# Conditioning vector and its row products begin within the first mixer, with a sum buffer of their own

## The chip, the core and the metric

One core of a Trainium2 chip runs the whole program. The metric is device time in microseconds (us) of one execution; the median of the runs counts. The engines are named as in the profile: PE is TensorE (PEld its weight loads), DVE VectorE, ACT ScalarE, POOL GpSimd, SP SyncE, whose queue issues most DMAs.

## What is computed

Two transformer blocks on 512 tokens of width 1024, in float32, one after the other:

```python
x = first_block(x, mem, ...)      # mixer (two attentions), cross attention, SwiGLU
x = second_block(x, c, ...)       # mLSTM mixer, squared-ReLU MLP, MLA mixer, squared-ReLU MLP
# in second_block
cond = jax.nn.silu(c)             # one vector of 1024
for l in range(2):
    ada = cond @ ada_w[l] + ada_b[l]               # 6 rows of 1024
    sh1, sc1, g1, sh2, sc2, g2 = jnp.split(ada, 6, axis=-1)
    ...
kv_shift, kv_scale = jnp.split(cond @ kv_ada_w + kv_ada_b, 2, axis=-1)
```

The 14 rows of 1024 (six per layer and two for the shared keys and values) depend on c and on weights alone, on nothing of the first block. They are first needed at the end of SwiGLU, and from there on until the last MLP.

## The kernel before

The stream x stays on chip. Each weight matrix comes in by SP's DMA queue, is split by ACT and DVE into a rounded high part and a low rest, and every product is three PE matmuls (high by high, high by low, low by high: `prod`, L440, lines L445 to L447). A wino product (L490) with seven instead of eight block products serves the later blocks of the squared-ReLU MLPs; it asks DVE for sums beside the splits. Instructions are written out in program order; a list scheduler then orders each engine's queue by that order and by its own estimate of when operands and buffers are there, and puts in the waits. On the chip each engine works its queue in that fixed order, so an instruction whose operand is late holds all behind it.

The stages in the order of time: first mixer (value projection, then 64 softmax tiles of `soft64` woven with projections, then the output projection) until 346 us, cross attention until 500, SwiGLU until 850, mLSTM until 1100, first squared-ReLU MLP until 1450, MLA until 1700, second squared-ReLU MLP until the end. Between two stages stands a `boundary` (L641), a chain over normalisation and transposes.

**The rows in the background.** `cond` (L793) loads c and makes silu(c) with a Tanh on ACT and two small DVE instructions. `ada` (L804) is a generator that makes the rows, each in two halves of 512 columns by `row_by` (L838). One half is nine steps: POOL clears a sum tile and fetches the bias (L843, L844); eight slices of weights (256 KB each) come into two `araw` slots by SP's queue (L856), and for each DVE does sum = slice * cond + sum (L852); DVE adds the two halves of the partitions (L860), ACT and DVE split the result into `hl` (L864); one PE matmul with ones adds up over the partitions (L869); DVE applies the gain (L882 or L886), and POOL sends the half row to DRAM (L888, shown as L201, the line of its helper). Two further half-width products (rows 14 and 15) and four fetches of a row as columns belong to the same generator. In all it has 278 steps.

`step` (L453) is called for each product of `prod`, at 0.65 units each, and advances the generator by one step when 3 units are used up (2.5 from the end of mLSTM on): every fifth (fourth) product. Within a boundary (`quiet`) it doesn't. Before `self.bg = self.ada()` it has nothing to advance. `crow` (L893) and `gcol` (L406) advance it at once where a row is needed and not there.

Buffers by tag: `u2` has 16 slots of 2 KB a partition for all kinds of tiles, `araw` 2, the 8 PSUM banks are `ps`. A tile waits for a free slot of its tag.

Of the kernel before, what the change touches and what calls it, by code (L numbers as in the profile page):

```python
# [10 lines left out]
F32 = mybir.dt.float32  # L11
F32R = mybir.dt.float32r
# [8 lines left out]
P = 128  # L21
# [9 lines left out]
D_FF = 2816  # L31
ALL = slice(0, S)

BUF = dict(s8=14, u2=16, row=3, raw=4, w0=4, w1=4, w2=4, w3=5, w4=5, w5=5, w6=5, w7=5, ps=8, pace=3, pacb=2.5, man=0, lag=3, lagx=3, lagm=3, half=1, quiet=1, xp=0, fp=2, r1=1.25, r1b=3.6, r1c=2.4, r2=1.6, r2b=2.6, rx=1.4, rm=0.6, pre=10, gl=3, pl=0, hb=300, hs=0, ha=0, sp=0, spq=1.3, sq=1, b1=1, b2=1, lc=7, mb=(6, 8, 6, 6, 6), mc=(4, 3, 4, 4, 4), st2=1, pr2=8, z1=4.5, z2=5, gt=3, rv=2, gs=1, rl=3, n1=4, ex=2, em=3, vg=1, sb=(8, 8, 6), mo=4, x1=2, g0=20, st=1, y1=0, y2=1, y3=0, ph=2, pq=0, fy=1, u1=6, s32=4, sm=60)

TWO_PI = 2.0 * np.pi

# [101 lines left out]
class Net:  # L139
# [27 lines left out]
    def big(self, shape, dt=F32):  # L167
        return self.t("s8", shape, dt, BUF["s8"])

    def u2(self, shape=(P, S), dt=F32):  # L170
        if BUF["u1"] and int(np.prod(shape[1:])) <= 256:
            return self.t("u1", shape, dt, BUF["u1"])
        return self.t("u2", shape, dt, BUF["u2"])

    def row(self, n=DM):
        return self.t("row", [P, n], F32, BUF["row"])

    def sm(self, n=1, p=P, dt=F32):
        if n > 8:
            return self.t("sm32", [p, n], dt, BUF["s32"])  # L180
        return self.t("sm", [p, n], dt, BUF["sm"])
# [656 lines left out]
    def row_by(self, i, c, ws, n, vec, b=None, gain=None, kind=0):  # L838

        nc, V = self.nc, self.nc.vector  # L840
        acc = self.u2((P, n))
        if b is not None:
            nc.gpsimd.memset(acc, 0.0)  # L843
            self.small(acc[0:1, :], b.rearrange("(o c) -> o c", o=1))  # L844
        yield
        raws = {}
        for k in range(0, KD + 2, 2):
            for j in (k, k + 1):
                if j == 2 and b is None:
                    V.tensor_scalar(out=acc, in0=raws.pop(0), scalar1=vec[:, 0:1], scalar2=None, op0=ALU.mult)  # L850
                elif j >= 2:
                    V.scalar_tensor_tensor(out=acc, in0=raws.pop(j - 2), scalar=vec[:, j - 2:j - 1], in1=acc,  # L852
                                           op0=ALU.mult, op1=ALU.add)
                if j < KD:
                    raws[j] = self.t("araw", [P, n], F32, 2)
                    nc.sync.dma_start(out=raws[j], in_=ws[:, j, :])  # L856
            yield
        if BUF["fy"]:
            h = P // 2
            (V if BUF["fy"] == 1 else nc.gpsimd).tensor_tensor(out=acc[0:h, :], in0=acc[0:h, :], in1=acc[h:P, :], op=ALU.add)  # L860
            hl = self.u2((P, n), F32R)
            for _ in range(BUF["y1"]):
                yield
            self.parts(hl[0:h, :], hl[h:P, :], acc[0:h, :])  # L864
            yield
            for _ in range(BUF["y2"]):
                yield
            ps = self.bank((P, n))
            nc.tensor.matmul(ps, lhsT=self.onesr, rhs=hl, start=True, stop=True)  # L869
        else:  # L870
            hi, lo = self.u2((P, n), F32R), self.u2((P, n), F32R)
            for _ in range(BUF["y1"]):
                yield
            self.parts(hi, lo, acc)
            yield
            for _ in range(BUF["y2"]):
                yield
            ps = self.bank((P, n))
            nc.tensor.matmul(ps, lhsT=self.onesr, rhs=hi, start=True, stop=False)
            nc.tensor.matmul(ps, lhsT=self.onesr, rhs=lo, start=False, stop=True)  # L880
        if gain is None:
            V.tensor_copy(out=acc[0:1, :], in_=ps[0:1, :])  # L882
        else:
            g = self.u2((1, n))
            self.small(g, gain.rearrange("(o c) -> o c", o=1))
            V.scalar_tensor_tensor(out=acc[0:1, :], in0=ps[0:1, :], scalar=1.0 if kind == 1 else 0.0,  # L886
                                   in1=g, op0=ALU.add, op1=ALU.mult)
        self.small(self.arow[i:i + 1, c:c + n], acc[0:1, :])  # L888
        if c or n < S:
            self.have.add(i)  # L890
        yield
# [157 lines left out]
    def mixer1(self):  # L1049
# [18 lines left out]
        with self.in_order():  # L1068
            self.mixer1_values(h, vf, w)
        self.cap(0)  # L1070

        wg = self.weights(w, 0, KD, 1536, 8, gain="mix")
        psg = self.bank()
# [44 lines left out]
        vs, os, st = [vf, None], [None, None], {}  # L1118
# [9 lines left out]
        def fill():  # L1128
            m = self.mem_in()
            for pair in range(8):  # L1130
                c = 0 if pair < 4 else 1544
                r = []
                if pair == 4:
                    self.cap(1)
                    yield from v_chunk()
                for i, y in enumerate(self.stacks(w, h, c + 512, c, pair % 4, 1.0, 0.125, r, "mix")):
                    if pair == 7 and i in (2, 9):
                        next(m)
                    yield y
                st[2 * pair], st[2 * pair + 1] = r  # L1140
            for _ in m:
                pass
            yield from self.mem_keys()
# [12 lines left out]
        f, gs = fill(), self.gains()  # L1156
# [33 lines left out]
        g = self.brow(a["g_mix_post"][0], eng=self.nc.sync)  # L1190
# [727 lines left out]
    def mixer1_and_tables(self):  # L1918
        r = self.mixer1()
        self.rope_tables()  # L1920
        self.cond()
        self.bg = self.ada()
        return r


# [34 lines left out]
```

## Time and profile before

| | |
|---|---|
| median of 3 runs | 2031.46 us (2030.95 to 2033.41) |
| the profiled execution: time | 2033.3 us |
| its span | 2031.5 us |
| PE, PEld busy in it | 1941.8 us (96%), 1665.1 us (82%) |
| DVE, ACT, POOL busy | 1396.7 us (69%), 1025.0 us (50%), 331.7 us (16%) |
| mean granted PE clock | 0.982 |

All that follows is of the one profiled execution; us in a row count from the start of its span. PE is near its peak over the span as a whole, so that what matters are the few places where it waits.

### The profile page before, as it was taken

The page shows a single profiled execution, that of the slowest core. Times are in us where ns is not written, and L with a number is a line of the kernel's source. Part 1 is how long each engine was busy: PE and PEld are TensorE (multiplying, and loading weights), DVE is VectorE, ACT ScalarE, POOL GpSimd, SP SyncE. Part 2 cuts the span into 40 slices and gives each one's busy share as a digit, 9 for nine tenths or more (in the row PEclk, how much of TensorE's full clock was granted, in tenths as well). Part 3 has the DMA queues.
Part 4 walks back from the last instruction along what each step waited for, and adds up shares of the span by engine and source line. Part 5 has one row for each costly group of instructions (what it writes and reads, how often), then busy time and mean ns, then how long its engine had stood idle before and what let it go on. Part 6 is the DMA issues. An engine that isn't in the chain of part 4 may idle for free.

```text
span 2031.5 us, 29708 instructions
## 1 busy us (share of the span) xinstructions
PE 1941.8 (96%) x10684; PEld 1665.1 (82%) x10684; DVE 1396.7 (69%) x2659; ACT 1025.0 (50%) x2283; POOL 331.7 (16%) x615
## 2 busy tenths in 40 slices
PE   8999998999999999999998899999979999999998
PEld 5888987778888888778888788798767978989987
DVE  5756645756576576757767897889758656657666
ACT  7767874545244233347534363454545644545444
POOL 1321113003000000421126100000330034000001
PEclk9999999999999999999999999999989999999999
DMA  7322341433465465244333355555342203233322
GB/s 219 89 79 76 118 129 61 137 104 103 157 202 159 137 203 142 83 142 129 120 104 113 117 163 156 183 167 159 102 134 89 73 12 103 83 104 115 103 74 83
DMA packets 191667, 245.14 MB, mean 121 GB/s; under 512 B 20059, under 2 KB 119488, under 8 KB 191520
## 3 DMA queue, kind: packets, MB, share of 16 engines
q1 hardware_dynamic: 185264, 232.15, 37.0%
q0 software_dynamic: 6256, 11.10, 1.9%
q8 instruction: 84, 1.38, 0.3%
q14 instruction: 63, 0.52, 0.1%
HBM read 241.00 MB, written 2.20 MB: 120 GB/s over the span
## 4 chain that ended last, share of the span: by engine, by line
PE 69%; DVE 14%; issue 6%; DMA 5%; ACT 4%; POOL 2%; DVEq 0%; POOLq 0%; ACTq 0%
PE ps L447 18%; PE ps L446 18%; PE ps L445 18%; PE ps L508 7%; DMA araw<-in_ada_w 3%; DVE u L852 2%; DVE s L308 2%; DVE s L318 2%; PE ps L1011 1%; DVE s L634 1%; DVE s L342 1%; DVE x L654 1%; ACT junk L579 1%; PE ps L1793 1%; PE ps L1822 1%
## 5 line engine op out<-in xcount | busy, mean ns | idle before, releaser
L445 PE MATMUL ps<-s,s 128*128 128x512 f32 (+4 forms) x2260 | 857.8, 383 | 8.4 <-ACT s L633 4.8
L446 PE MATMUL ps<-s,s 128*128 128x512 f32 (+4 forms) x2260 | 850.5, 377 | 12.2 <-DVE s L634 11.9
L447 PE MATMUL ps<-s,s 128*128 128x512 f32 (+4 forms) x2260 | 845.2, 377 | 4.7 <-DVE s L634 4.6
L446 PEld LDWEIGHTS ps<-s,s 128*128 128x128 f32 (+1 forms) x2260 | 431.7, 191 | 90.0 <-DVE s L634 13.7
L447 PEld LDWEIGHTS ps<-s,s 128*128 128x128 f32 (+1 forms) x2260 | 430.2, 190 | 86.7 <-DVE s L634 7.4
L445 PEld LDWEIGHTS ps<-s,s 128*128 128x128 f32 (+1 forms) x2260 | 429.7, 191 | 84.9 <-ACT s L633 7.5
L508 PE MATMUL ps<-s,s 128*128 128x256 f32 x2184 | 265.3, 282 | 10.0 <-DVE u L524 6.9
L508 PEld LDWEIGHTS ps<-s,s 128*128 128x128 f32 x2184 | 262.8, 189 | 13.8 <-issue 5.9
L852 DVE SCALAR_TENSOR_TENSOR u<-araw,cond,u 128x512 f32<-128x512 f32 x224 | 177.2, 791 | 108.6 <-DMA araw<-in_ada_w 87.2
L308 DVE TENSOR_TENSOR s<-raw,s 128x512 fp32r<-128x512 f32 x277 | 193.3, 736 | 42.5 <-ACT s L307 37.0
L307 ACT ACTIVATE s<-raw 128x512 fp32r<-128x512 f32 x255 | 144.9, 622 | 152.8 <-PE ps L447 96.4
L317 ACT ACTIVATE s<-raw,cols_all 128x256 fp32r<-128x256 f32 (+1 forms) x283 | 134.2, 547 | 47.5 <-issue 22.1
L318 DVE SCALAR_TENSOR_TENSOR s<-raw,cols_all,s 128x256 fp32r<-128x256 f32 (+1 forms) x305 | 150.5, 546 | 8.7 <-ACT s L317 7.3
L201 POOL DMA_DIRECT2D arow<-u x30 | 14.7, 492 | 629.6 <-DVE u L886 378.9
L568 POOL TENSOR_SCALAR sm<-sm 128x1 f32<-128x1 f32 x74 | 20.5, 277 | 558.9 <-ACT junk L579 556.1
L634 DVE TENSOR_TENSOR s<-ps,s 128x512 fp32r<-128x512 f32 (+3 forms) x124 | 75.2, 619 | 40.6 <-ACT s L633 39.7
L341 ACT ACTIVATE s<-raw 128x512 fp32r<-128x512 f32 x104 | 62.6, 621 | 67.9 <-PE ps L447 32.9
L634 DVE TENSOR_TENSOR s<-u,s 128x512 fp32r<-128x512 f32 x102 | 69.7, 686 | 39.4 <-ACT s L633 35.8
L633 ACT ACTIVATE s<-u 128x512 fp32r<-128x512 f32 x102 | 63.6, 625 | 64.0 <-DVE u L1403 49.3
L633 ACT ACTIVATE s<-ps 128x512 fp32r<-128x512 f32 (+3 forms) x124 | 65.2, 538 | 38.3 <-PE ps L626 16.1
L341 ACT ACTIVATE s<-u 128x512 fp32r<-128x512 f32 x78 | 48.7, 624 | 61.0 <-DVE u L345 31.6
L342 DVE TENSOR_TENSOR s<-raw,s 128x512 fp32r<-128x512 f32 x104 | 70.5, 682 | 11.0 <-ACT s L341 10.9
(264 smaller groups left out, 2211.7 us busy)
## 6 DMA issues: line engine op xcount, KB each, us to landing
raw<-in_mlp_w SPq DMA_DIRECT2D x128, 512.0 KB, 4.0
araw<-in_ada_w SPq DMA_DIRECT2D x192, 256.0 KB, 3.0
raw<-in_w_gate_up SPq DMA_DIRECT2D x44, 512.0 KB, 4.3
raw<-in_w_in SPq DMA_DIRECT2D x24, 512.0 KB, 4.6
raw<-in_a_w_in SPq DMA_DIRECT2D x24, 512.0 KB, 4.0
raw<-in_w_down SPq DMA_DIRECT2D x22, 512.0 KB, 4.1
raw<-in_w_mem_kv SPq DMA_DIRECT2D x16, 512.0 KB, 3.6
araw<-in_kv_ada_w SPq DMA_DIRECT2D x32, 256.0 KB, 3.1
```

Of the source, the lines that this page charges most:

```text
L307: A.activation(hi[:, sl, cl], src[:, sl, cl], AF.Copy)
L308: f.tensor_tensor(out=lo[:, sl, cl], in0=src[:, sl, cl], in1=hi[:, sl, cl].bitcast(F32), op=ALU.subtract)
L317: A.activation(hi[:, i, :], src[:, i, :], AF.Copy, scale=g)
L318: V.scalar_tensor_tensor(out=lo[:, i, :], in0=src[:, i, :], scalar=g, in1=hi[:, i, :].bitcast(F32), op0=ALU.mult, op1=ALU.subtract)
L341: A.activation(hi, x, AF.Copy)
L445: self.nc.tensor.matmul(ps, lhsT=ah, rhs=bh, start=first and i == 0, stop=False)
L446: self.nc.tensor.matmul(ps, lhsT=ah, rhs=bl, start=False, stop=False)
L447: self.nc.tensor.matmul(ps, lhsT=al, rhs=bh, start=False, stop=last and i == n - 1)
L508: nc.tensor.matmul(ps, lhsT=l[:, k, :], rhs=m[:, k, :], start=first and k == e == 0, stop=k == 3 and e == 2, skip_group_check=True)
L633: self.nc.scalar.activation(hi, x, AF.Copy)
L634: self.nc.vector.tensor_tensor(out=lo, in0=x, in1=hi.bitcast(F32), op=ALU.subtract)
L852: V.scalar_tensor_tensor(out=acc, in0=raws.pop(j - 2), scalar=vec[:, j - 2:j - 1], in1=acc, op0=ALU.mult, op1=ALU.add)
```

## The change

`cond()` is called, and the generator set up, within the first mixer right behind the value projection, and no longer after the mixer and the rope tables. The sum tile of `row_by` gets a tag of its own, `ua`, with one slot; `hl` and the gain slice `g` now take slots of `araw`, beside the weight slices; `u2` has 15 slots instead of 16. What is computed stays the same.

```diff
--- before.py
+++ after.py
@@ -31,7 +31,7 @@
 D_FF = 2816
 ALL = slice(0, S)
 
-BUF = dict(s8=14, u2=16, row=3, raw=4,
...
+BUF = dict(s8=14, u2=15, row=3, raw=4,
...
 
 TWO_PI = 2.0 * np.pi
 
@@ -838,7 +838,7 @@
     def row_by(self, i, c, ws, n, vec, b=None, gain=None, kind=0):
 
         nc, V = self.nc, self.nc.vector
-        acc = self.u2((P, n))
+        acc = self.t("ua", [P, n], F32, 1)
         if b is not None:
             nc.gpsimd.memset(acc, 0.0)
             self.small(acc[0:1, :], b.rearrange("(o c) -> o c", o=1))
@@ -858,7 +858,7 @@
         if BUF["fy"]:
             h = P // 2
             (V if BUF["fy"] == 1 else nc.gpsimd).tensor_tensor(out=acc[0:h, :], in0=acc[0:h, :], in1=acc[h:P, :], op=ALU.add)
-            hl = self.u2((P, n), F32R)
+            hl = self.t("araw", [P, n], F32R, 2)
             for _ in range(BUF["y1"]):
                 yield
             self.parts(hl[0:h, :], hl[h:P, :], acc[0:h, :])
@@ -881,7 +881,7 @@
         if gain is None:
             V.tensor_copy(out=acc[0:1, :], in_=ps[0:1, :])
         else:
-            g = self.u2((1, n))
+            g = self.t("araw", [1, n], F32, 2)
             self.small(g, gain.rearrange("(o c) -> o c", o=1))
             V.scalar_tensor_tensor(out=acc[0:1, :], in0=ps[0:1, :], scalar=1.0 if kind == 1 else 0.0,
                                    in1=g, op0=ALU.add, op1=ALU.mult)
@@ -1068,6 +1068,8 @@
         with self.in_order():
             self.mixer1_values(h, vf, w)
         self.cap(0)
+        self.cond()
+        self.bg = self.ada()
 
         wg = self.weights(w, 0, KD, 1536, 8, gain="mix")
         psg = self.bank()
@@ -1918,8 +1920,6 @@
     def mixer1_and_tables(self):
         r = self.mixer1()
         self.rope_tables()
-        self.cond()
-        self.bg = self.ada()
         return r
 
 
```

## Rows read from the trace of the kernel before

**Rows 1.** The page, part 2: the span in 40 slices, the busy share of PE in tenths.

```profile
PE   8999998999999999999998899999979999999998
```

**Rows 2.** The waits of PE over the whole span: who waited for whom, us in total, times, longest.

```profile
PE ps L869 <- DVE u L634: 17.0, 4, 6.4
PE ps L508 <- DVE u L524: 6.9, 3, 5.8
```

**Rows 3.** Windows over stages: the window and its length in us, then busy us and instructions of PE, PEld, DVE, ACT and POOL, the granted PE clock, the busy share of the DMA engines, GB/s. In order: first mixer up to its boundary, SwiGLU, mLSTM, the first squared-ReLU MLP in two parts, the start of MLA, the second squared-ReLU MLP.

```profile
50.00:318.00 268.00, 266.06 (x1579) 232.35 (x1578) 156.52 (x402) 188.03 (x484) 57.52 (x164) 1.00 0.32 93
500.00:850.00 350.00, 350.00 (x1527) 285.01 (x1526) 233.62 (x399) 132.17 (x282) 36.65 (x66) 1.00 0.51 154
900.00:1050.00 150.00, 150.00 (x773) 126.20 (x772) 113.22 (x227) 82.39 (x190) 24.46 (x34) 1.00 0.45 139
1100.00:1305.00 205.00, 189.66 (x1165) 168.69 (x1166) 168.46 (x271) 97.56 (x179) 23.72 (x35) 0.98 0.49 153
1305.00:1450.00 145.00, 136.03 (x823) 121.04 (x822) 121.81 (x207) 67.27 (x129) 8.69 (x17) 0.98 0.50 152
1495.00:1560.00 65.00, 55.35 (x280) 47.41 (x278) 52.72 (x126) 33.60 (x80) 9.26 (x19) 0.95 0.42 126
1700.00:2024.00 324.00, 324.00 (x2015) 290.20 (x2013) 209.25 (x358) 160.30 (x301) 11.37 (x15) 1.00 0.28 90
```

**Rows 4.** The timeline of PE at five places: start us, us, line, operation, output and inputs, shape, and in brackets the idle time before it in us and what ended it.

```profile
1138.42 0.79 PE L869 MATMUL ps<-u,onesr 128*128 128x512 f32 x1 [5.21 <-DVE u L634]
1167.51 0.51 PE L869 MATMUL ps<-u,onesr 128*128 128x512 f32 x1 [1.24 <-DVE u L634]
1286.91 0.63 PE L869 MATMUL ps<-u,onesr 128*128 128x512 f32 x1 [4.15 <-DVE u L634]
1425.78 0.55 PE L508 MATMUL ps<-s,s 128*128 128x256 f32 x1 [5.77 <-DVE u L524]
1517.10 0.79 PE L869 MATMUL ps<-u,onesr 128*128 128x512 f32 x1 [6.44 <-DVE u L634]
```

**Rows 5.** Windows (columns as in rows 3) from the end of four of those waits to the place where the granted clock is 1.00 again.

```profile
1138.42:1143.77 5.35, 5.35 (x13) 4.19 (x14) 5.35 (x9) 3.94 (x8) 0.00 (x0) 0.50 0.00 0
1286.91:1290.54 3.63, 3.62 (x9) 2.85 (x10) 3.63 (x7) 0.00 (x0) 0.49 (x1) 0.53 0.80 262
1425.78:1430.49 4.71, 4.71 (x17) 4.32 (x18) 3.30 (x6) 1.23 (x2) 0.38 (x1) 0.50 0.78 247
1517.10:1522.65 5.55, 5.55 (x16) 4.49 (x17) 2.31 (x4) 3.89 (x7) 2.81 (x6) 0.50 0.30 100
```

**Rows 6.** Windows for line L869 alone, the row sum that ends each half: busy us and count of PE and PEld, then the clock, DMA share and GB/s of the window.

```profile
0.00:346.00 346.00, 0.00 (x0) 0.00 (x0) 0.99 0.37 112
346.00:850.00 504.00, 4.74 (x12) 2.26 (x12) 0.99 0.45 138
850.00:1100.00 250.00, 1.89 (x5) 0.94 (x5) 0.98 0.41 127
1100.00:1305.00 205.00, 3.05 (x6) 1.22 (x6) 0.98 0.49 153
1305.00:1560.00 255.00, 3.41 (x7) 1.56 (x7) 0.96 0.45 136
```

**Rows 7.** The timeline of PE in SwiGLU: two row sums that follow one another.

```profile
573.36 0.40 PE L869 MATMUL ps<-u,onesr 128*128 128x512 f32 x1
604.77 0.39 PE L869 MATMUL ps<-u,onesr 128*128 128x512 f32 x1
```

**Rows 8.** The window of the first mixer for line L447 alone, the last of the three matmuls of a product: busy us and count of PE and PEld.

```profile
35.00:318.00 283.00, 118.29 (x317) 58.85 (x317) 1.00 0.32 93
```

**Rows 9.** The instructions of a half. Line L852 by its own view (ns min/median/max, first and last start); the others from the groups by line and form (count, busy us, mean ns, idle before in us and what ended it).

```profile
L852 DVE SCALAR_TENSOR_TENSOR u<-araw,cond,u x224: 729/750/10624, 352.1 to 1539.4; 128x512 f32<-128x512 f32 x112
...
  DMA araw<-in_ada_w: 87.2, 69
...
L634 DVE TENSOR_TENSOR u<-u,u 64x512 fp32r<-64x512 f32 x28 | 20.2, 720 | 2.0 <-ACT u L633 1.3
L860 DVE TENSOR_TENSOR u<-u 64x512 f32<-64x512 f32 x28 | 19.2, 687 | 0.9
L886 DVE SCALAR_TENSOR_TENSOR u<-ps,u 1x512 f32<-1x512 f32 x18 | 12.1, 673 | 2.6 <-PE ps L869 1.3 <-DMA u<-in_norm_g 1.2
L843 POOL MEMSET u<- 128x512 f32 x28 | 15.1, 540 | 51.9 <-DVE s L634 34.6 <-DVE s L342 17.3
```

**Rows 10.** DMA issues: queue, count, KB each, median us from issue to landing.

```profile
arow<-u POOLq DMA_DIRECT2D x28, 2.0 KB, 1.6
u<-in_ada_b POOLq DMA_DIRECT2D x24, 2.0 KB, 2.7
```

**Rows 11.** The waits of the SP queue: us in total, times, longest.

```profile
SPq L856 <- DVE u L852: 248.5, 201, 19.1
```

**Rows 12.** The timeline of DVE and of POOL at 1114 us (x is how many are merged in the row), and the views of lines L1097 and L1099, which make the biases of the first mixer on POOL.

```profile
1113.78 12.19 DVE L852 SCALAR_TENSOR_TENSOR u<-araw,cond,u 128x512 f32<-128x512 f32 x3
...
1114.55 10.07 POOL L480 TENSOR_TENSOR u<-s 128x512 f32<-128x512 f32 x8
...
L1097 POOL TENSOR_SCALAR u<-u,sm x32: 367/574/1120, 65.8 to 155.3; 128x128 f32<-128x128 f32 x8, 128x384 f32<-128x384 f32 x8, 128x256 f32<-128x256 f32 x8, 128x512 f32<-128x512 f32 x8
...
L1099 POOL TENSOR_SCALAR_AFFINE_SELECT u<-u x32: 283/294/613, 66.9 to 156.0; 128x128 f32<-128x128 f32 x32
```

More of the change, by code (lines that the diff above doesn't have):

```diff
@@ L32 @@
 ALL = slice(0, S)
-BUF = dict(s8=14, u2=16, row=3, raw=4, w0=4, w1=4, w2=4, w3=5, w4=5, w5=5, w6=5, w7=5, ps=8, pace=3, pacb=2.5, man=0, lag=3, lagx=3, lagm=3, half=1, quiet=1, xp=0, fp=2, r1=1.25, r1b=3.6, r1c=2.4, r2=1.6, r2b=2.6, rx=1.4, rm=0.6, pre=10, gl=3, pl=0, hb=300, hs=0, ha=0, sp=0, spq=1.3, sq=1, b1=1, b2=1, lc=7, mb=(6, 8, 6, 6, 6), mc=(4, 3, 4, 4, 4), st2=1, pr2=8, z1=4.5, z2=5, gt=3, rv=2, gs=1, rl=3, n1=4, ex=2, em=3, vg=1, sb=(8, 8, 6), mo=4, x1=2, g0=20, st=1, y1=0, y2=1, y3=0, ph=2, pq=0, fy=1, u1=6, s32=4, sm=60)
+BUF = dict(s8=14, u2=15, row=3, raw=4, w0=4, w1=4, w2=4, w3=5, w4=5, w5=5, w6=5, w7=5, ps=8, pace=3, pacb=2.5, man=0, lag=3, lagx=3, lagm=3, half=1, quiet=1, xp=0, fp=2, r1=1.25, r1b=3.6, r1c=2.4, r2=1.6, r2b=2.6, rx=1.4, rm=0.6, pre=10, gl=3, pl=0, hb=300, hs=0, ha=0, sp=0, spq=1.3, sq=1, b1=1, b2=1, lc=7, mb=(6, 8, 6, 6, 6), mc=(4, 3, 4, 4, 4), st2=1, pr2=8, z1=4.5, z2=5, gt=3, rv=2, gs=1, rl=3, n1=4, ex=2, em=3, vg=1, sb=(8, 8, 6), mo=4, x1=2, g0=20, st=1, y1=0, y2=1, y3=0, ph=2, pq=0, fy=1, u1=6, s32=4, sm=60)
 TWO_PI = 2.0 * np.pi
```

## The prediction

> **What bounds the kernel now.** I read the slices of the page first: PE is at nine or ten tenths nearly everywhere, so the time is PE's own work plus a few holes [rows 1]. The waits of PE name the largest one: row sums of the background (L869) that wait for their split, 17.0 us in four waits; the single longest of the rest is a wino product that waits for DVE (L524) [rows 2]. Windows by stage then tell where the background hurts. In SwiGLU it runs and PE is busy 350.00 of 350 us; in mLSTM 150.00 of 150; in the first squared-ReLU MLP with it PE is idle 15.3 us up to 1305 us and 9.0 us more up to 1450; in the second such MLP, which runs after the background's end, PE is busy 324.00 of 324 us [rows 3]. The difference between the two MLPs is on DVE: 82% and 84% busy in the first (168.5 of 205, 121.8 of 145), 65% in the second (209.3 of 324) [rows 3].
>
> A wait also costs after its end: behind four of the long waits the granted clock stands at 0.50 (that is 1.2 GHz instead of 2.4) for 3.6 to 5.6 us [rows 5], and PE does half its work in that time. So the wait at 1517 us costs 6.44 + 5.55 / 2 = 9.2 us [rows 4, 5].
>
> **How far the rows move.** In SwiGLU two row sums lie 604.77 - 573.36 = 31.4 us apart [rows 7]. That is nine steps of five products, 31.4 / 45 = 0.70 us a product, just as the code counts. In the first mixer, `prod` runs behind the new place of `ada()` for 8 (forget gate) + 128 (stacks) + 32 (chunk values) + 64 (memory keys) + 32 (memory values) + 32 (first half of the output projection) = 296 products; the trace has 317 of the last matmul between 35 and 318 us [rows 8], 8 of the value projection and some 13 of the quiet second half of the output projection included, which fits. 296 / 5 = 59 steps, or 6.5 halves, are then done before cross attention begins; from there on the pace is what it was. Today's row sums stand at 0 before 346 us, 12 up to 850, 5, 6 up to 1305, and 7 from there to 1560 [rows 6]. I expect 6 before 346, the next three counts about the same, and none behind some 1305 us: step 278 comes where now step 219 is. No row is needed earlier than it is there, so nothing else moves with it.
>
> **What it takes away.** The wait at 1517 us with its slow clock, 9.2 us. In 1305 to 1450 the idle 9.0 us and the slow clock behind 1425.78, 4.71 / 2 = 2.4 us, together 11.3 [rows 3 to 5]: four halves of 8.1 us of DVE (below) leave that window, and DVE falls from 121.8 to about 89.5 of 145 us, 62%, below the 65% of the second MLP that never waits. What is late next: in the MLP nothing; in MLA the transposes and the splits of weights that now queue behind the same row sum, for which I take 2 us back. Gain 20.5 - 2 = 18.5 us.
>
> **What it adds in the first mixer.** A half costs DVE 8 x 0.750 + 0.687 + 0.720 + 0.673 = 8.1 us [rows 9], and PE one matmul, which is only moved. ACT gets one split of a half, POOL a memset and two or three DMA issues, SP eight loads of 256 KB, on DMA engines that are 32% busy there [rows 3]. Six halves bring DVE from 156.5 to 205 of 268 us, 76.5% [rows 3]. Three queues matter. DVE: a product with a late slice holds the softmax maxima and the weight splits behind it (now 87.2 us in 69 waits over all [rows 9]). SP: a load that waits for an `araw` slot (248.5 us, longest 19.1 [rows 11]) holds the weight loads of the mixer's projections. POOL: the issue of the finished half waits for DVE, and behind it stand the attention biases (L1097, L1099 [rows 12]). PE is covered: the softmax runs three tiles ahead and the stacks 26 steps. The trace has no mixer with the background in it, so I bound the price from both sides. From below it is 0, as in SwiGLU and mLSTM. From above it is the rate of 1100 to 1305 us: 15.3 us idle and (5.35 + 3.63) / 2 = 4.5 of slow clock for six halves, 3.3 a half, 21.5 for 6.5 [rows 3, 5, 6]. By DVE's share 76.5% is next to mLSTM's 75.5% (113.2 of 150) and far from 82.2%; between these ends the straight line gives 1.0 / 6.7 x 21.5 = 3.2 us, which I take. `cond` itself (one load, one Tanh, two small DVE instructions) is nothing beside this, and its old place at 346 us is no wait that the next stage depends on, since the rope tables stay there.
>
> **What the buffers add.** With one `ua` slot a half's memset waits until the previous half has landed in DRAM: 0.67 (L886) + 1.6 (landing) + 0.54 (memset) + 2.7 (bias) = 5.5 us from the row sum to the first product [rows 9, 10]. The program leaves three steps for it, 10.5 us, or 8.4 in the late pace of four products: hidden. Where half-width products make steps shorter (once, at 1100 us) up to 5.5 us may show; and `hl` and the gain slice in `araw` keep the next two slices from being fetched ahead. From 0 to 5.5 us, I take 2. For `u2`, 15 slots instead of 16: the sum tile, `hl` and the gain slice took up to three of the 16 in SwiGLU, where PE did not wait; so the others live on 13 to 15 already. POOL's 51.9 us of waits for a slot before the memset [rows 9] end; they held nobody that PE waited for. I take 0, with 4 us either way. The three waits that lie before 1305 us [rows 4] meet other halves than now; I leave them as they are.
>
> Sum: -18.5 + 3.2 + 2 = -13.3 us. The profiled execution takes 2033.3 us (span 2031.5) and would come to 2020.0; the median of the runs, 2031.46, comes to 2018.
>
> **The rivals.**
>
> VectorE falls behind in the mixer (slower). Its queue is in order, and a row sum stands in PE's queue at a fixed place. If every half in the mixer ends as the four waits for L869 do, it costs (5.21 + 1.24 + 4.15 + 6.44) / 4 = 4.3 us and (5.35 + 3.63 + 5.55) / 2 / 4 = 1.8 of slow clock, 6.1 a half [rows 4, 5], 36.5 for six: -18.5 + 36.5 + 2 = +20, 2051 us. It decides from (18.5 - 2) / 6 = 2.8 us a half on. For it speaks that PE has no reserve in that stage (266.1 of 268 us busy); against it SwiGLU and mLSTM, where the same halves cost nothing. 15%.
>
> GpSimd holds VectorE. At 1114 us three products took 12.2 us on DVE while eight additions ran on POOL for 10.1 us [rows 12]; the usual product takes 0.75. The first mixer is the stage with the most such company: 64 bias instructions (32 x 0.574 + 32 x 0.294 = 27.8 us) between 66 and 156 us. If each of some 15 products there waits out one of 0.574 us, DVE has 9 us more, 79.8%, and the line above gives 13.8 instead of 3.2 us: -2.7 in all, 2029 us. The trace shows long holds only behind two-input additions, not behind these one-input instructions. 8%. The Trainium skill, SBUF — State Buffer, section "Who interferes with whom", states a rule that speaks against this change: a DVE instruction with two SBUF inputs, as these products are, contends with any GpSimd instruction that reads SBUF, and whichever is second blocks. By that rule this rival holds, with the bias instructions as well; the row at 1114 us agrees with the rule for additions.
>
> Half of the gain is taken up by waits that come next in MLA and the MLP: -9.2 + 5.2 = -4, 2027.5 us. DVE at 62% speaks against it. 10%.
>
> More goes: the three waits before 1305 us vanish too, since other steps now meet the quarters and wino products and the sum tile no longer waits for a `u2` slot: 5.21 + 2.7 + 1.24 + 4.15 + 1.8 = 15.1 us [rows 4, 5], 2003 us. Speaks for it: the half at 1138 met POOL's additions by chance of phase. 9%.
>
> The generator doesn't advance in the mixer, so that only buffers change: 2031 us. The step counter runs there already, so 2%.
>
> **How the numbers follow.** The forecast of 2018 us has 56%; its own range, from the bounds of the mixer's price, the buffers and what is late next, is 2010 to 2027. Two runs of this kernel can be told apart from about 0.2%, 4 us: faster is below 2027.4, slower above 2035.5. Faster: 56 + 9 + half of 10 = 70%. Same: 5 + 8 + 2 = 15%. Slower: 15%. The range leaves out the slow rival and little else, and goes down to where the three waits vanish: 2004 to 2037.
>
> **What would show it.** Row sums: 6 before 346 us and none behind 1320. The first mixer's window to 318 us longer by no more than 9 us, PE idle in it by no more than 5. In the MLA start no wait at L869; in the first MLP's last 150 us PE nearly without idle time and DVE near 62%. Wrong would be: waits of PE at L869 or at softmax transposes in the first mixer, at 2.8 us a half or more; or new waits of the weight splits behind SP.

## The result: slower by 1.1 %

The changed kernel takes 2054.59 us (median; 2053.69 to 2056.06) against 2032.43 us before on the same chip (2030.95 to 2033.5), ratio 1.011, 95 % interval 1.0093 to 1.0128. Its profiled execution takes 2054.55 us, with a span of 2052.6 us. Behind line 1070 the lines of the changed kernel stand two further down (L1097 and L1099 are L1099 and L1101); those of the rows (L843 to L886) are where they were. In the runs below they keep their numbers too, unless the text says otherwise.

The forecast was 2018 us and faster. The rows did move as forecast: six row sums lie before 372 us (the mixer now ends there), the last one at 1355 us. The time did not follow. The slices of the page, the same row as in [rows 1]:

```profile
PE   7999999898999999999998969799999998999998
```

The lowest slice was the thirtieth (the start of MLA); it is now the twenty-fourth (1180 to 1232 us), with the twenty-sixth next to it. The waits of PE, to be set against [rows 2]:

```profile
PE ps L869 <- DVE araw L634: 27.4, 5, 13.8
...
PE ps L995 <- ACT u L1002: 4.0, 1, 4.0
PE ps L1011 <- ACT u L997: 3.9, 2, 2.0
...
PE ps L508 <- DVE u L524: 1.7, 2, 1.4
```

The largest wait, for the row sum's split, has grown from 17.0 to 27.4 us instead of shrinking. Two waits in the softmax of the first mixer stand out: that of its transposes (L995) was 0.9 us before, and that of its values (L1011) is new. The windows of [rows 3], with the same columns and limits:

```profile
50.00:318.00 268.00, 251.58 (x1474) 218.18 (x1473) 187.83 (x451) 187.73 (x478) 70.32 (x180) 0.97 0.42 125
...
500.00:850.00 350.00, 349.61 (x1596) 288.16 (x1597) 214.84 (x390) 128.75 (x270) 20.07 (x40) 0.99 0.48 149
900.00:1050.00 150.00, 150.00 (x767) 124.32 (x765) 106.73 (x214) 81.56 (x185) 24.91 (x36) 1.00 0.43 130
1100.00:1305.00 205.00, 176.47 (x1074) 156.91 (x1073) 157.42 (x237) 85.66 (x161) 42.49 (x54) 0.93 0.44 136
1305.00:1450.00 145.00, 134.53 (x843) 121.33 (x843) 102.89 (x177) 66.11 (x124) 2.95 (x6) 0.98 0.38 117
1495.00:1560.00 65.00, 60.11 (x333) 54.49 (x333) 44.56 (x105) 36.65 (x86) 22.93 (x42) 0.97 0.40 118
```

The mixer's window holds 14.5 us less of PE's work and a clock of 0.97. SwiGLU and mLSTM carry the rows almost for nothing, as before. The start of the first MLP (1100 to 1305) has become the worst place: idle 28.5 us where 15.3 were. The MLA window is better (60.1 for 55.4), as forecast.

Windows are fixed in time while the work shifts, so the rest of this text uses landmarks as well: the start of the last update of x (L654 on DVE) at the end of each stage, read from the timeline of that line. In us, the kernel before, and the difference to it:

```
                    mixer  SwiGLU  mLSTM  1st MLP    MLA  last
before              343.8   862.1 1086.1  1478.9  1681.9 2027.5
after               +26.4   +27.8  +27.6   +34.5   +21.3  +21.1
start moved alone   +25.4   +29.5  +31.6   +14.6    +0.5   +2.8   (e1)
buffers alone        +1.9    +5.2   +5.7   +23.6   +16.9  +17.0   (e2)
rows from tile 8    +12.9   +12.5  +13.1    -7.3   -21.4  -19.4   (n3)
tiles 8 to 42 only   +1.8    -1.1   +4.2    -6.2   -19.7  -18.1   (m1)
from tile 8, all three buffer changes
                    +18.1   +22.9  +23.3   +36.3   +22.4  +24.2   (z4)
from tile 8, two sum slots
                    +15.7   +14.8  +16.0    -5.8   -19.5  -17.7   (v1)
```

Each row is of one traced execution; that of m1 was its fastest (2015.22 us for a median of 2022.62), so its row is some 7 us too good. The changed kernel loses 26 us in the mixer, loses 7 in the first MLP where it should have won, and wins 13 in MLA.

### The profile page after: what moved, and what is told of

The parts are those of the page before. It is cut to its first block, busy times and chain, and to the rows that moved or that the text cites. A ratio compares the mean times of both kernels' runs of the same rounds, so it can differ in the third digit from the quotient of the medians.

```text
span 2052.6 us, 29764 instructions
## 1 busy us (share of the span) xinstructions
PE 1947.8 (95%) x10684; PEld 1668.5 (81%) x10684; DVE 1394.6 (68%) x2659; ACT 1022.5 (50%) x2281; POOL 336.0 (16%) x615
## 5 line engine op out<-in xcount | busy, mean ns | idle before, releaser
L446 PE MATMUL ps<-s,s 128*128 128x512 f32 (+4 forms) x2260 | 851.1, 377 | 11.3 <-DVE s L634 11.1
L447 PE MATMUL ps<-s,s 128*128 128x512 f32 (+4 forms) x2260 | 847.6, 377 | 7.5 <-DVE s L634 7.5
L447 PEld LDWEIGHTS ps<-s,s 128*128 128x128 f32 (+1 forms) x2260 | 430.5, 191 | 90.2 <-DVE s L634 10.4
L445 PEld LDWEIGHTS ps<-s,s 128*128 128x128 f32 (+1 forms) x2260 | 429.9, 191 | 85.6 <-ACT s L633 10.7
L852 DVE SCALAR_TENSOR_TENSOR ua<-araw,cond,ua 128x512 f32<-128x512 f32 x224 | 176.2, 787 | 163.4 <-DMA araw<-in_ada_w 76.4
L634 DVE TENSOR_TENSOR s<-ps,s 128x512 fp32r<-128x512 f32 (+3 forms) x124 | 75.1, 619 | 38.5 <-ACT s L633 37.5
L633 ACT ACTIVATE s<-u 128x512 fp32r<-128x512 f32 x102 | 63.5, 625 | 67.6 <-DVE u L1405 40.8
L634 DVE TENSOR_TENSOR s<-u,s 128x512 fp32r<-128x512 f32 x102 | 69.5, 685 | 40.2 <-ACT s L633 37.9
L201 POOL DMA_DIRECT2D arow<-ua x30 | 15.2, 507 | 430.6 <-DVE ua L882 241.5
L633 ACT ACTIVATE s<-ps 128x512 fp32r<-128x512 f32 (+3 forms) x124 | 64.9, 538 | 37.5 <-PE ps L626 18.0
L342 DVE TENSOR_TENSOR s<-raw,s 128x512 fp32r<-128x512 f32 x104 | 70.5, 682 | 14.6 <-ACT s L341 14.0
```

The costliest lines, as they stand in the source:

```text
L445: self.nc.tensor.matmul(ps, lhsT=ah, rhs=bh, start=first and i == 0, stop=False)
L446: self.nc.tensor.matmul(ps, lhsT=ah, rhs=bl, start=False, stop=False)
L447: self.nc.tensor.matmul(ps, lhsT=al, rhs=bh, start=False, stop=last and i == n - 1)
L633: self.nc.scalar.activation(hi, x, AF.Copy)
L634: self.nc.vector.tensor_tensor(out=lo, in0=x, in1=hi.bitcast(F32), op=ALU.subtract)
```

## Two places where the time went

**The start of the softmax.** The timeline of DVE in the changed kernel, the products of the first half (L852) and the forget gate's chain (L905, L907, the scan L1079); in brackets the idle time before an instruction and its cause:

```profile
44.18 0.75 DVE L852 SCALAR_TENSOR_TENSOR ua<-araw,cond,ua 128x512 f32<-128x512 f32 x1 [1.30 <-DMA araw<-in_ada_w]
...
47.59 0.75 DVE L852 SCALAR_TENSOR_TENSOR ua<-araw,cond,ua 128x512 f32<-128x512 f32 x1 [1.42 <-DMA araw<-in_ada_w]
49.07 0.75 DVE L852 SCALAR_TENSOR_TENSOR ua<-araw,cond,ua 128x512 f32<-128x512 f32 x1 [0.73 <-DMA araw<-in_ada_w]
49.74 0.73 DVE L905 TENSOR_SCALAR u<-ps,sm 8x512 f32<-8x512 f32 x1
...
51.11 0.67 DVE L907 SCALAR_TENSOR_TENSOR u<-u 8x512 f32<-8x512 f32 x1
...
58.40 1.21 DVE L1079 TENSOR_TENSOR_SCAN u<-ones,u 8x512 f32<-8x512 f32 x1
```

and of PE, the first transposes of the softmax, in the changed kernel and in the kernel before, then the window around them in the changed kernel:

```profile
74.39 0.47 PE L995 MATMUL ps<-ident,u 128*128 128x128 f32 x1 [4.02 <-ACT u L1002]
```

```profile
70.55 0.33 PE L995 MATMUL ps<-ident,u 128*128 128x128 f32 x1 [0.86 <-ACT u L1002]
```

```profile
72.30:79.10 6.80, 4.71 (x13) 3.84 (x14) 5.53 (x14) 5.34 (x14) 2.62 (x6) 0.50 0.69 194
```

In the kernel before the same chain stands at 46.39 (L905), 47.16 (L907) and 52.62 (the scan, there L1077):

```profile
46.39 0.74 DVE L905 TENSOR_SCALAR u<-ps,sm 8x512 f32<-8x512 f32 x1 [6.66 <-PE ps L447]
...
52.62 1.21 DVE L1077 TENSOR_TENSOR_SCAN u<-ones,u 8x512 f32<-8x512 f32 x1
```

It is now 3.4, 4.0 and 5.8 us late. DVE is not short of time there: from 44.18 on it stands idle for 3.9 us in front of four products that wait for their 256 KB slice, and its queue is in order. The exponentials (L1002) get the delay through ACT's queue: ACT waits at a copy of the stacks (L953) for DVE's part of them (L955), which stands behind the gate's chain, and from that copy to the exponential it is busy without a gap. ACT in the changed kernel, then in the kernel before:

```profile
65.79 0.60 ACT L953 ACTIVATE u<-ps 64x512 fp32r<-64x512 f32 x1 [3.64 <-DVE u L955]
...
73.84 0.40 ACT L1002 ACTIVATE u<-u,sm 128x128 f32<-128x128 f32 x1
```

```profile
61.94 0.59 ACT L953 ACTIVATE u<-ps 64x512 fp32r<-64x512 f32 x1 [2.38 <-DVE u L955]
...
70.00 0.40 ACT L1002 ACTIVATE u<-u,sm 128x128 f32<-128x128 f32 x1
```

Copy, exponential and transpose are all 3.8 us late. PE waits 4.0 us, and the granted clock is 0.50 (1.2 GHz) over the 6.8 us of the window.

**The start of each half.** The view of L852, what its engine waited for (us, times):

```profile
  DMA araw<-in_ada_w: 76.4, 84
  DMA ua<-in_ada_b: 53.5, 17
  DMA araw<-in_kv_ada_w: 14.9, 14
  DMA ua<-in_kv_ada_b: 13.6, 4
```

67.1 us in 21 waits are for the bias that goes into the sum tile; before it was 4.2 us in two. The longest wait of PE, 13.84 us, has this chain. DVE:

```profile
1177.47 0.67 DVE L886 SCALAR_TENSOR_TENSOR ua<-ps,araw 1x512 f32<-1x512 f32 x1
...
1187.23 0.75 DVE L852 SCALAR_TENSOR_TENSOR ua<-araw,cond,ua 128x512 f32<-128x512 f32 x1 [3.68 <-DMA ua<-in_ada_b]
...
1202.39 0.69 DVE L860 TENSOR_TENSOR ua<-ua 64x512 f32<-64x512 f32 x1
...
1205.11 0.69 DVE L634 TENSOR_TENSOR araw<-ua,araw 64x512 fp32r<-64x512 f32 x1
```

POOL, between the first two of these:

```profile
1178.43 0.49 POOL L201 DMA_DIRECT2D arow<-ua  x1 [10.25 <-DVE ua L886]
1183.40 0.53 POOL L843 MEMSET ua<- 128x512 f32 x1 [4.47 <-DMA arow<-ua]
1184.21 0.48 POOL L201 DMA_DIRECT2D ua<-in_ada_b  x1 [0.29 <-POOL ua L843]
```

PE, and the window of the slow clock around it:

```profile
1205.85 0.80 PE L869 MATMUL ps<-araw,onesr 128*128 128x512 f32 x1 [13.84 <-DVE araw L634]
```

```profile
1195.30:1208.90 13.60, 3.05 (x13) 2.96 (x14) 10.03 (x16) 3.56 (x6) 0.48 (x1) 0.50 0.49 155
```

With one slot the next half's memset waits until the finished half has landed in DRAM (4.47 us), the bias follows, and the first product stands 9.8 us behind L886. The fold L860 comes 15.2 us after that, and PE, which came to the row sum at 1192.0, waits for it.

## The experiments

A difference in us given behind a ratio is that ratio less one, times 2031.5; others are landmarks. Each ratio has its 95 % interval. "At equal PE work" means: at the time at which PE has done as much as in the kernel before, its busy time counted with the granted clock.

**The change in parts.** e1 is the kernel before with `cond()` and `ada()` moved and its old buffers; e2 has the old start and the three buffer changes; e3 changes only the shared pool; e4 is the changed kernel with two slots for the sum:

```diff
 e1: the hunks at 1068 and 1918 of the change alone
 e2: the other hunks alone
 e3: u2=16 -> u2=15 alone
 e4: the whole change, and
-        acc = self.t("ua", [P, n], F32, 1)      u2=15
+        acc = self.t("ua", [P, n], F32, 2)      u2=14
```

> Three theories for the 22 us. One sum slot: with a single ua slot a half can't be cleared before the last one has landed, VectorE then waits in order for the bias, and PE for the row sum. Mixer load: the work of the rows in the first mixer itself holds its softmax and splits, about 26 us up to the mixer's end. u2 short: 15 slots instead of 16 hold the softmax tiles. This kernel moves the start of the rows and keeps the old buffers (sum, split and gain in u2, 16 slots). One sum slot: the mixer loses under 8 us, the gain of 18 stays, 2015 to 2026. Mixer load: the mixer ends 20 us or more later, MLA gains, 2035 to 2045. u2 short: 2015 to 2026, and in the mixer the sum tiles take slots, so somewhat more.

> The new buffers (ua with one slot, split and gain in araw, u2 with 15) with the old start behind the mixer. One sum slot: slower than before by the waits for the bias in the first MLP and MLA, 2042 to 2055, VectorE waiting 50 us or more for the bias. Mixer load: 2030 to 2036. u2 short: mixer longer by 10 us or more though no rows run there, 2042 or more.

> The kernel before with u2 at 15 slots and nothing else. u2 short: 2040 or more, with the first mixer longer. One sum slot and mixer load: 2029 to 2036.

> The changed kernel with two slots for ua; the 2 KB come from u2, which has 14. One sum slot: the waits for the bias fall from 67 us to under 15 and the time to 2025 to 2038. Mixer load: 2045 to 2055, the mixer as late as in the changed kernel. u2 short: 2058 or more.

Measured: e1 0.999 (0.9979 to 1.0001), e2 1.007 (1.0055 to 1.0085), e3 1.0006 (0.9996 to 1.0016), e4 1.0031 (1.002 to 1.0041). The shared pool's slot costs nothing. The move alone is no gain: 25.4 us lost in the mixer and 6 more up to mLSTM, 31.1 won behind it (+31.6 at mLSTM, +0.5 at MLA). The buffers cost 14 us alone and 24 under the move (by the ratios of the changed kernel and of e1; 18 by the last landmarks); two slots take 16 of these back (e4, by the ratios), and behind mLSTM e4 wins 28.6 us, as much as e1 (28.8 to the last landmark). So neither theory alone: the mixer eats the gain, and the sum slot makes the loss.

**Where in the mixer.** m1 starts the rows at softmax tile 8 and holds them from tile 42 to the old place; n3 starts them at tile 8 and lets them run; n1 is m1 with a step every three products; z1 starts them just ahead of the softmax, behind the gate's chain. All have the old buffers.

```diff
 in the loop over the tiles of soft64 (m1; n3 without the last two lines)
+            if s == 8:
+                self.cond()
+                self.bg = self.ada()
+            if s == 42:
+                self.held, self.bg = self.bg, None
 mixer1_and_tables (m1: self.bg = self.held; n3, z1: neither line)
-        self.cond()
-        self.bg = self.ada()
 n1: BUF["pace"] = 1.9 at s == 8, 3 again at s == 42
 z1: cond() and ada() behind cc[0] = self.cols(c)
```

> Buffers as before. The rows start inside the first mixer, but only at softmax tile 8 (some 95 us), and are held from tile 42 to the end of the mixer, where they go on from the old place; so some 3 to 4 halves are done in the mixer, none of them in the chain that starts the softmax or in its tail. Theory 'edges' (the 25 us of the move alone sit at the softmax's start and tail, where a row instruction that waits for its load holds an instruction of the chain): the end of the mixer moves by under 6 us, the later stages give back some 17 us for 3.5 of 6.5 halves (31 x 3.5 / 6.5), net -10 to -15 us beside the kernel before. Rival 'load' (each half costs the mixer its share, 25 / 6.5 = 3.9 us): the mixer +13 us, net about -3 us, no difference.

> Old buffers; the rows start at softmax tile 8 as in the run with the middle alone, but are not held from tile 42 on: some 5 to 6 halves in the mixer, the tail of the softmax included, its start left out. Theory 'edges': the tail alone costs the mixer 9 to 16 us (the middle alone cost 1.4), the late stages give some 27; net -8 to -18 us, no better than the middle alone (-12.6). Rival 'phase' (the waits in the tail of the moved kernel were a chance of where its steps fell): the mixer under +5 us and the net -20 us or better. Rival 'load' (about 3.9 us a half): the mixer +20 us or more, which the middle alone already speaks against.

> Old buffers; the rows run between softmax tiles 8 and 42 alone, but with a step every three products there instead of every five, so some 5 halves lie in the middle instead of 3. Theory 'edges' (the middle has slack): the end of the mixer moves by under 5 us, and the late stages give some 25 us; net -18 us or better. Rival 'load' (what decides is how much of VectorE the rows take; at this pace it is near full): the mixer +10 us or more, and the net no better than with the ordinary pace there.

> Old buffers; the rows start behind the columns of the forget gate's sums, at the softmax's first tile, some 30 us of issue later than in the move and 8 tiles earlier than in the run from tile 8 on. Theory 'forget gate' (products in front of the scan delay the first bias): the 9 us at 65 to 76 us are gone, the mixer costs about what the start from tile 8 costs it (10 to 13 us, all in the tail), net -15 to -22 us. Rival 'first tiles' (the products in front of the first maxima hold them, wherever the gate's chain is): the 9 us stay, net near 0.

Measured: m1 0.9938 (0.9918 to 0.9957), n3 0.989 (0.9869 to 0.9911), n1 0.9948 (0.9932 to 0.9964), z1 0.9945 (0.9923 to 0.9966). In m1 two halves end in the mixer (a third is under way) and its end moves by 1.8 us; in n3 five end there, at 12.9 us, and nearly all of that falls behind 200 us. With the start at the head it is 25.4: at equal PE work e1 loses 8 us up to 100 us, nothing from there to 200, and 14 from 200 to 320. So the price depends on the place, as "edges" says; head and tail both cost, and in e1 the tail is the larger part. But two points went against it: n3 is better than m1, since the tail's 11 us buy more behind it; and n1 is 10.7 us late at the mixer's end with three halves ended there, not the five expected, so the middle has slack for the ordinary pace only. z1 is a miss for "forget gate" alone: its mixer is 2 us longer than n3's, and it loses 6 us between 76 and 97 us (at equal PE work), where DVE and PE show

```profile
85.48 1.00 DVE L852 SCALAR_TENSOR_TENSOR u<-araw,cond,u 128x512 f32<-128x512 f32 x1 [3.68 <-DMA araw<-in_ada_w]
86.40 0.28 DVE L985 CUSTOM_DVE_ANT_0 u<-ps,u 128x128 f32<-128x128 f32 x1
...
91.14 0.42 DVE L985 CUSTOM_DVE_ANT_0 u<-ps,u 128x256 f32<-128x256 f32 x1
```

```profile
91.72 0.45 PE L995 MATMUL ps<-ident,u 128*128 128x128 f32 x1 [2.77 <-DVE sm L985]
```

a row maximum (L985) at 86.40 for 83.99 before, behind a product that waits 3.68 us for its slice: another victim of a late slice. The next maximum, the one that PE waits for, stands at 91.14 for 85.60 before; another product, the fold and weight splits stand between, so the rows' own work adds to the wait. In the tail the delay passes through ACT. From e1, DVE, ACT, PE:

```profile
262.19 0.75 DVE L852 SCALAR_TENSOR_TENSOR u<-araw,cond,u 128x512 f32<-128x512 f32 x1 [1.44 <-DMA araw<-in_ada_w]
...
267.62 0.69 DVE L860 TENSOR_TENSOR u<-u 64x512 f32<-64x512 f32 x1
```

```profile
268.34 0.63 ACT L633 ACTIVATE u<-u 64x512 fp32r<-64x512 f32 x1 [2.84 <-DVE u L860]
268.88 0.95 ACT L997 ACTIVATE u<-ps 128x384 f32<-128x384 f32 x2
```

```profile
269.40 1.54 PE L1011 MATMUL ps<-s,u 128*128 128x64 f32 x6 [4.85 <-ACT u L997]
```

ACT's split of the half (L633) waits 2.84 us for the fold on DVE (L860), the softmax's copies (L997) stand behind it, and PE waits 4.85 us for these. DVE is busy without a gap from the product at 262.19 to that fold, 5.4 us with three products among them: in the tail, too, the rows' own work adds to the waiting.

**The wait for the load taken away.** x1 is e1 with 15 shared slots and products that read a constant tile; it leaves the loaded weights out of these rows, so that no product waits for a load:

```diff
-                    V.scalar_tensor_tensor(out=acc, in0=raws.pop(j - 2), ...
+                    raws.pop(j - 2)
+                    V.scalar_tensor_tensor(out=acc, in0=self.fix[:, 0:n], ...
```

> The moved start with the old buffers (15 in the shared pool, one given to a constant tile); the products of the conditioning rows multiply that constant tile instead of the loaded weight slice, so the rows' values are not the reference's. The loads are still issued, 256 KB each, and the products keep their number, shape and place, but none waits for a load any more, nor does a load wait for a product. Theory 'wait for the load held in order': the mixer's extra time falls from 25 us (the move alone) to under 8 us, and the late stages still give back some 30 us. Rival 'VectorE's own work' (the 8.1 us of a half are what costs): the mixer stays at +18 us or more. Rival 'traffic' (the loads delay the weight loads): also +18 or more.

Measured: 1.0113 (1.0098 to 1.0128). The total is a miss: the mixer ends 39.6 us late. It still tells two things. At 76 us, where e1 is 7.6 us late at equal PE work, x1 is 0.2 late, with the same eight products on DVE, and its gate's chain begins at 46.34 us (46.39 before); the wait, not the work, costs at the start. And the loads, no longer paced by products, took SP's queue. SP and ACT (here the row load is L862):

```profile
136.80 17.85 SPq L862 DMA_DIRECT2D araw<-in_ada_w  x13
154.70 0.43 SPq L421 DMA_DIRECT2D raw<-in_w_in  x1
```

```profile
159.00 2.16 ACT L317 ACTIVATE s<-raw,cols_mix 128x128 fp32r<-128x128 f32 x7 [16.09 <-DMA raw<-in_w_in]
```

A weight load was issued behind 13 row loads, and ACT stood 16.09 us. That is a new fault of this run, not one of the changed kernel; so behind the start x1 does not part the wait from the work. From 200 to 320 us it loses 7.0 us at equal PE work where e1 loses 14, though no product waits for a load.

**The buffers apart.** g1 puts only the split and the gain slice into the loads' slots; g2 only the sum tile into one slot (15 shared); z5 the sum tile into two (14 shared); x2 is e2 with the finished half in a tile of the shared pool, so that the sum slot is free before the landing:

```diff
 g1: the two lines with "araw" of the change alone
 g2: acc = self.t("ua", [P, n], F32, 1), u2=15 alone
 z5: acc = self.t("ua", [P, n], F32, 2), u2=14 alone
 x2: e2, and ahead of "if gain is None"
+        acc = self.u2((1, n))
```

> Old start; the split sum and the gain slice move into the two slots of the loads, the sum tile stays in the shared pool with its 16 slots. All three buffer changes together cost 14 to 17 us. Theory 'one sum slot' (the next half's memset and bias wait until the last sum has landed): this part alone costs under 4 us. Rival 'load slots' (the split holds one of two load slots while the next half's first loads want it, so the first products come late): 10 us or more, with waits of the products for their loads longer than before and waits of PE at the row sums.

> Old start; only the sum tile moves, into a single slot of its own, and the shared pool has 15 slots; the split sum and the gain slice stay in the shared pool. Theory 'one sum slot': most of the 14 to 17 us, 10 or more, with products that wait for the bias (53.5 us in the changed kernel). Rival 'load slots': under 4 us, since the loads then run ahead of the wait for the bias; an even split (5 to 9 us each) would say that only the two waits in a row reach PE.

> Old start; the sum tile has two slots of its own, the shared pool 14, split sum and gain slice stay in the shared pool. Theory 'single slot' (the wait for the one slot is what cost 28 us): within 4 us of before. Rival 'phase' or 'fewer shared slots': +10 us or more in spite of the second slot.

> Old start with all three buffer changes (+14 to +17 us so far), but the finished half goes out of a tile of the shared pool, so that the single sum slot is free when the split has read it, and not only when the finished half has landed. Theory 'one sum slot, held until the landing': the products' waits for the bias fall from 65 us to under 20, and the kernel comes within 5 us of before. Rival 'load slots' (the split and the gain slice hold the two slots of the loads): still +7 us, what these alone cost. Rival 'late bias' (even so the memset and the bias come after the first step): +10 us or more, with bias waits over 40 us.

Measured: g1 1.0034 (1.002 to 1.0048), g2 1.0156 (1.0126 to 1.0185), z5 0.9974 (0.9961 to 0.9987), x2 1.006 (1.0045 to 1.0075). One sum slot alone costs 32 us, more than all three buffer changes together (14); two slots cost nothing. x2 is a miss for the landing alone: its waits for the bias fall from 64.8 us to 1.9, and its price only from 14 to 12. That its memset still needs the split of the half before (L634; POOL waits 226.8 us for it in 26 waits), and its loads the shared slots of g1, fits this; it was not separated further. Where e2 lost, the landing did count: in the first MLP x2 loses 5.5 us by the landmarks for e2's 17.9, and PE waits 6.5 us at row sums for 32.4. But x2 loses 9.0 us in SwiGLU, where e2 loses 2.5, and why is open.

**How much is chance of phase.** z6 shifts the rows by three empty steps; z4 is the changed kernel with n3's start; v1 is n3 with z5's sum slots.

```diff
 z6: at the head of ada()
+        for _ in range(3):
+            yield
 z4: the change with n3's start       v1: z5 with n3's start
```

> The kernel before with three empty steps ahead of the first row, so that every row sum stands 15 products later, some 10 us, and nothing else differs. Theory 'each part has its own price': within 4 us of before. Rival 'phase': 6 us or more either way, and then no difference of that size between two runs with old start can be put down to a part.

> The kernel after the change with one thing different: the rows start at softmax tile 8 instead of at the head of the mixer. Theory 'parts add': the late start alone took 20 us off (2014) and the three buffers add 14 to 20, so 2028 to 2034, within 0.4 % of before. Rival 'phase' (the buffers' price depends on where the row sums fall): outside 2020 to 2040.

> Rows from softmax tile 8 on, the sum tile in two slots of its own, 14 shared slots, split sum and gain slice in the shared pool. Theory 'one slot makes each half start late': between 1130 and 1350 us the first product comes within 5 us of the row sum in most halves, and the kernel stands within 6 us of the late start with the old buffers (2014), so 2008 to 2020, against 2056.7 with the changed kernel's buffers. Rival 'a slot of its own, or fewer shared slots, costs too': 2025 us or more.

Measured: z6 0.9965 (0.9949 to 0.9981), z4 1.0089 (1.0065 to 1.0113), v1 0.9879 (0.9861 to 0.9896). A shift alone is worth 7 us, so g1's +7 and z5's -5 are not told apart from it; g2's +32 and z4 against n3 (1.0089 against 0.989) are. z4 fell to the rival: parts do not add. By the ratios the buffers cost 14 us with the old start, 24 with the early one and 40 with the late one (17, 18 and 44 by the last landmarks).

What does agree over the kernels is when a half begins. Between 1130 and 1330 us, from the start of a row sum (L869, timeline of PE) to the first product (L852, or L850 in a half without a bias) behind that half's fold (L860, timelines of DVE), us, and the mean; a negative one began ahead of the row sum:

```
before               7.8  8.2 -1.1 -6.5 12.5  3.7 -3.0   mean  3.1
z5, two slots       -2.8 10.8 -5.3 -8.6 -11.9 -17.9 -17.6 mean -7.6
v1, two slots       -2.8 -5.9  7.2  8.0  9.7 -15.6 -10.9 mean -1.5
n3, old buffers      8.4  2.2  9.9 -2.6 -5.1  4.9 -0.4   mean  2.5
g1, old sum tile     9.1  7.9  6.1  3.3 15.9  4.5  7.6   mean  7.8
after, one slot      7.5 15.1  6.3  8.1  8.1 10.1  7.7   mean  9.0
g2, one slot         7.8 11.6  8.9 12.6  7.4 12.5        mean 10.1
z4, one slot        14.9  8.6  6.2  8.1 10.2  8.4        mean  9.4
x2, slot free early 12.1  8.1  3.4  3.2  6.2  3.4        mean  6.1
```

With one slot held until the landing no half begins sooner than 6.2 us behind the last row sum; with two slots or the old buffers many begin ahead of it. A half of the changed kernel has 27 to 34 us from sum to sum there, so 9.0 us is more than a quarter of its time. But a late start is not the price by itself: in g1 no half begins ahead either, and g1 costs 7 us, no more than a shift. Nor is DVE's waiting: in z5 it waits 39.0 us for biases in 16 waits, and z5 costs nothing. In e2 and g2, where the slot costs, PE waits 32.4 and 29.7 us at row sums, for 17.0 before and none in z5 and v1; z4, with 14.6, does not follow this.

**More pace behind the mixer.** h1 leaves start and buffers and sets `pace=2.4` for 3, a step every four products.

> Start and buffers as before; behind the mixer a step of the rows is taken every four products instead of every five, so 219 steps x 5/4 = 274 of some 278 are done where 219 are done now, and the last row sum comes near 1305 us without any half in the mixer. Theory 'mixer edges' (the move loses in the mixer what it gains in the late stages, and SwiGLU and mLSTM can carry more halves): the late stages give some 25 to 31 us, cross attention, SwiGLU and mLSTM lose under 10, net -15 to -30 us. Rival 'conservation' (a half costs PE about 4 us wherever it runs, only the place changes): -4 to +4 us.

Measured: 0.9969 (0.9955 to 0.9983), 6 us, between the theories: its mLSTM landmark is 18.0 us late (in the traced execution, at 2035.14 us its slowest), so mLSTM does not carry more halves for nothing, and the last row sum stands at 1392.5 us, not 1305.

**A better version** is n3, the move with its start at tile 8 and the old buffers: 2014.04 us, 0.989. Two sum slots (v1, 2013.10) are no better than the old buffers there. Its window over the start of the first MLP, to be set against the two above and in [rows 3]:

```profile
1100.00:1305.00 205.00, 196.99 (x1258) 178.15 (x1258) 172.07 (x273) 97.09 (x183) 36.52 (x49) 0.98 0.52 159
```

PE is busy 197.0 us of 205 there with DVE at 84 %, a higher share than the changed kernel's 77 %, where PE is busy 176.5.

## Why the prediction was wrong, step by step

**How far the rows move** was right: six row sums in the mixer, the last at 1355 for some 1305, where the changed kernel itself is some 30 us late.

**The gain** was right in its mechanism and too small: 18.5 us forecast, 31.1 measured in e1 behind mLSTM (17.0 in the first MLP, 14.1 in MLA). Forecast were 11.3 for the first MLP's end and 9.2 for MLA, less 2 for what comes next; nothing came next. At equal PE work e1 wins 10.3 us between 1304 and 1450 us, about as forecast for that stretch; MLA's 14.1 are more than the 9.2; and of the 27.1 us that e1 is late at 1100 and the 31.0 at 1170, 24.0 are left at 1304, a stretch that the prediction left as it was.

**The mixer's price** is the first step that failed: 3.2 us forecast, 25.4 measured in e1, beyond the bound of 21.5 as well. It was sized by DVE's share, and share is not what costs. The share came to 70 % (187.8 of 268), lower than the 76.5 % forecast, mLSTM carries the rows at 71 % (106.7 of 150) with PE busy all the time, and n3 in the first MLP at 84 % for 8 us of idle time; in the mixer's own window n3 has DVE at 72 % (194.2 of 268) and loses half of what e1 loses. At the head what costs is a product that waits for its slice in an in-order queue ahead of an instruction of the softmax's chain, where that chain has no reserve: without that wait 7.4 of e1's 7.6 us are gone (x1). In the tail, where e1 loses 14, such waits are there too, but they were not parted from the rows' own work on DVE. The prediction did name that queue ("a product with a late slice holds the softmax maxima"), but then took PE as covered "three tiles ahead": at the head of the softmax nothing is ahead yet, and the gate's chain was not looked at.

**What the buffers add** is the second: 2 us forecast, 18 to 24 measured between e1 and the changed kernel. The chain was taken as 5.5 us and "hidden" in three steps of 10.5. It measured 9.8 us at 1177 us, where the memset stood 4.47 us for the landing; the prediction had the median of 1.6 in [rows 10]. And hiding it in the steps left out what the kernel before had: three of its seven halves between 1130 and 1330 us begin ahead of the last row sum, and with one slot held until the landing none does. The price of the slot is shown (g2, z5, e4); that the lost head start alone makes it is not (g1). POOL, whose waits before the memset [rows 9] were read as harmless, stood there 5 times before and stands 23 times for the landing now, 58.1 us.

**The shared pool**, 0 with 4 either way, was right (e3, 0.9996 to 1.0016).

**The rivals.** "VectorE falls behind in the mixer" gave 2051 us and has the right side and stage, but not its mechanism: of six halves there only one row sum made PE wait (2.3 us at 272.9); the waits are those of the softmax. About half of the loss against the forecast is the buffers, for which no rival ended slower. "GpSimd holds VectorE" showed at 0.7 us of its 9: the 15 products between 66 and 156 us took 12.0 us, 797 ns each for 750 in SwiGLU. Seven of them overlap a bias instruction in the trace; four of these took 782 to 1082 ns, the other three 734 to 751, and the eight without an overlap 732 to 753. By the Trainium skill, SBUF — State Buffer, section "Who interferes with whom", in each overlap the one that issues second should block. The trace agrees for four of the seven; for the other three it does not tell which issued first, as spans on POOL are rough.

**What stays open.** The tail, 9 us in n3 and 14 in e1 at equal PE work from 200 to 320 us, was traced at single waits only, and no run frees the tail alone. Why g2 costs more than e2 is not settled beyond the 7 us of phase that z6 shows. Of the 40 us between z4 and n3, 9.5 are PE's waits at row sums (14.6 and 5.1); the rest was not followed.

## What to carry to other kernels

Before work is moved into a stage, read the chain that starts that stage and ask, for each in-order queue, which of its instructions would stand behind a moved one that waits for its own load; a share of busy time does not answer that. Before a rotating buffer gets a single slot, measure how early the next round begins today against the event that will free the slot: that head start is lost. And test the parts together, since here the same buffers cost 14, 24 and 40 us at three starts.

## What the hardware showed unasked

Row loads into two slots with no reader are each issued when the load before them in the same slot has landed: 13 loads of 256 KB took 17.85 us of SP's queue in x1, 1.37 us each, and everything behind them on SP waited. The landing of a 2 KB store from POOL, 1.6 us in the median before, held the next memset for 4.47 us at 1178 us in the changed kernel, whose median is 2.6 us:

```profile
arow<-ua POOLq DMA_DIRECT2D x28, 2.0 KB, 2.6
```
